# Storing one 4 MiB block in two transfers of 16 KB rows instead of one of 32 KB rows

## Chip, cores and metric

One core of one Trainium2 chip runs the program. The metric is the device time of one execution in microseconds (us). The span of a profile is about 1.3 us shorter than the time of the same execution.

## The reference

A DoRA forward pass: a 256 x 256 weight is adapted by a product of rank 16, its columns are normalised and scaled, and a large x is multiplied by it.

```python
W_adapted = W + scale * (lora_A @ lora_B)                      # 256 x 256
W_norm = np.sqrt(np.sum(W_adapted ** 2, axis=0, keepdims=True) + 1e-8)
W_final = W_adapted / W_norm * m
y = x.reshape(-1, 256) @ W_final                               # 32768 x 256, fp32 in and out
```

x and y are 33.6 MB each. They are what the time goes into.

## The kernel before

x is cut into 8 blocks of 4096 rows (32 KB a partition, 4 MiB). Five block buffers hold x on the chip. A block has 8 groups; a group g is one product of 512 rows, and its result is written by ScalarE over x in the same buffer. Loads are issued by the sync engine, stores by ScalarE. Each entry of `stores` is (first group, groups, rows of 1 KB in one transfer, product behind which it is issued).

```python
F = NBLK - XBUFS          # 3
G = F * CH                # 24: first group of block 3
stores = [(b * CH, CH, CH * J, 19 + b) for b in range(F - 1)]           # blocks 0, 1
stores += [(G - CH, 3, 3 * J, G), (G - 5, 5, 5 * J, G)]                 # block 2
FIRST = len(stores)
stores += [(G, 4, J, G + 3), (G + 4, 1, J, G + 4)]                      # block 3: rows of 4 KB
stores += [(G + 5, CH - 5, (CH - 5) * J, 44), (G + CH, CH, CH * J, 44)] # rest of 3; block 4
stores += [(b * CH, CH, CH * J, (b + 1) * CH - 1) for b in range(F + 2, NBLK - 1)]  # 5, 6
stores += [(g0, cnt, cnt * J, g0 + cnt - 1) for g0, cnt in units[-2:]]  # two halves of 7
# ... (transfer cuts an entry into pieces and issues each)
    for r in range(0, cnt * J, rows):
        here = x_bufs[b % XBUFS][:, c * J + r : c * J + r + rows, :]
        there = unit[:, (g0 - u0) * J + r : (g0 - u0) * J + r + rows, :]
        src, dst = (here, there) if store else (there, here)
        engine.dma_start(out=dst, in_=src).then_inc(sem(name), 16)
# ... (ScalarE, for each g)
    nc.scalar.copy(out=x_bufs[b % XBUFS][:, c * J : (c + 1) * J, :], in_=y_ps[g % 2][:])  # ...
    due = [n for n in range(len(stores)) if stores[n][3] == g]
    if due:
        nc.scalar.drain().then_inc(sem("done"), 1)   # ... then waits for it
        for n in due:
            store_y(n)
# ... (the end: the sync engine waits for the late stores)
for k, s in enumerate(late):
    nc.sync.wait_ge(s, pieces(stores[FIRST + k]))
```

Of the kernel before, what the change touches and what calls it, by code (L numbers as in the profile page):

```python
# [11 lines left out]
def kernel(  # L12
# [23 lines left out]
    J = 4  # L36
# [7 lines left out]
    CH = DJ // J  # L44
# [64 lines left out]
    G = F * CH  # L109
# [6 lines left out]
    stores = [(b * CH, CH, CH * J, 19 + b) for b in range(F - 1)]  # L116
    stores += [(G - CH, 3, 3 * J, G), (G - 5, 5, 5 * J, G)]
    FIRST = len(stores)
    stores += [(G, 4, J, G + 3), (G + 4, 1, J, G + 4)]
    stores += [(G + 5, CH - 5, (CH - 5) * J, 44), (G + CH, CH, CH * J, 44)]  # L120
    stores += [(b * CH, CH, CH * J, (b + 1) * CH - 1) for b in range(F + 2, NBLK - 1)]
    stores += [(g0, cnt, cnt * J, g0 + cnt - 1) for g0, cnt in units[-2:]]

# [272 lines left out]
```

## Time and profile before

| | before |
|---|---|
| time, median of 3 runs | 162.8 us (162.69 to 162.82) |
| span of the profile | 161.3 us |
| share of the DMA engines' span, loads and stores | 49.2% and 48.9% |
| last issue by ScalarE | 131.15 us |
| landing of block 4, of the last store | 132.1 us, 161.2 us |

Three things have to be known to read what follows. The DMA row of the slices gives the mean busy share of the 16 DMA engines in tenths. In a timeline the columns are the start in us, the duration in us, the engine, the source line, the operation, the operands, how many were merged, and in brackets the idle time before and what ended it. In a DMA view "us to landing" runs from an issue to the moment when all 16 engines have told that their part is written. The prediction shows the lines themselves.

### The profile page before, as it was taken

To read this page: it belongs to the slowest core of one execution; us is meant where nothing else is said; L and a number is where in the kernel's file an instruction comes from. 1 tells how busy PE (TensorE), PEld (TensorE's weight loads), DVE (VectorE), ACT (ScalarE), POOL (GpSimd) and SP (SyncE) were. 2 spreads that over 40 slices of the span, in tenths; PEclk is the share of its full clock that TensorE was granted. 3 is DMA by queue.
4 is the path that set the end of the run, shared out by engine and by line. 5 is a ranking of instruction groups with operands and counts; after the bars stand their busy time and mean duration, and the time that the engine had idled before them with its cause. 6 is when DMAs were issued, how large, how long until landed. Compare 5 with 4: busy or idle time off the path is not lost. (4 is left out here: it accounts for less than half of the span.)

```text
span 161.3 us, 2027 instructions
## 1 busy us (share of the span) xinstructions
PE 96.0 (60%) x786; PEld 84.8 (53%) x786; DVE 45.0 (28%) x44; ACT 66.0 (41%) x68; POOL 60.9 (38%) x38
## 2 busy tenths in 40 slices
PE   0795936999999720000799999989997920000000
PEld 0384925899998610000689999979977910000000
DVE  0667421435353500000214445335443300000000
ACT  3311740686777450000057676777774640000000
POOL 1045319668685000002938676755829000000000
PEclk9999996999999985555569999999999997555555
DMA  4999999999999999989999999999999999999995
GB/s 167 425 457 455 390 512 398 390 512 398 423 390 480 398 463 426 431 365 453 423 403 444 407 437 427 422 423 430 443 483 398 423 473 408 406 480 415 386 443 219
DMA packets 4645, 67.43 MB, mean 418 GB/s; under 512 B 657, under 2 KB 674, under 8 KB 1698
## 3 DMA queue, kind: packets, MB, share of 16 engines
q1 hardware_dynamic: 2304, 33.82, 49.2%
q10 hardware_dynamic: 2338, 33.59, 48.9%
q14 instruction: 3, 0.02, 0.0%
HBM read 33.85 MB, written 33.55 MB: 418 GB/s over the span
## 5 line engine op out<-in xcount | busy, mean ns | idle before, releaser
L276 ACT COPY x_sb<-y_ps 128x1024 f32<-128x1024 f32 x64 | 62.2, 1015 | 58.8 <-PE y_ps L335 57.1
L208 POOL CAST xb<-x_sb 128x2048 bf16<-128x2048 f32 x31 | 58.4, 1893 | 63.5 <-DMA x_sb<-in_x_dram 24.8
L335 PE MATMUL y_ps<-w_final,xt 128*128 128x256 bf16 x512 | 64.1, 279 | 3.9 <-PEq L311 3.8
L248 DVE COPY xt<-xt_ps 128x1024 f32<-128x1024 f32 x32 | 39.1, 1224 | 75.1 <-PE xt_ps L321 75.0
L335 PEld LDWEIGHTS y_ps<-w_final,xt 128*128 128x128 bf16 x512 | 51.0, 100 | 11.5 <-issue 4.9
L321 PE MATMUL xt_ps<-identity,xb 128*128 128x128 f32 x264 | 37.5, 290 | 24.9 <-PEq L311 24.9
L321 PEld LDWEIGHTS xt_ps<-identity,xb 128*128 128x128 f32 x264 | 32.8, 151 | 26.4 <-issue 25.9
L292 PE MATMUL y_ps<-identity,a_nat 128*16 128x128 f32 x2 | 0.6, 398 | 4.2 <-DMA a_nat<-in_lora_A_dram 4.2
L264 ACT CAST xb<-x_sb 128x2048 bf16<-128x2048 f32 x1 | 1.9, 1898 | 2.6 <-DMA x_sb<-in_x_dram 2.6
L292 PEld LDWEIGHTS y_ps<-identity,a_nat 128*16 128x16 f32 x2 | 0.1, 88 | 4.1 <-issue 4.1
L262 ACT ACT_TABLE_LOAD x1 | 1.3, 1283 | 2.4 <-issue 2.4
L238 DVE RECIPROCAL rnorm<-norm 128x256 f32<-128x256 f32 x1 | 1.8, 1752 | 1.3 <-ACT norm L268 1.3
L305 PE MATMUL y_ps<-sq,ones 128*128 128x256 f32 x4 | 2.1, 675 | 0.0
L214 POOL MEMSET xb<- 128x2048 bf16 x1 | 1.8, 1805 | 0.0
L305 PEld LDWEIGHTS y_ps<-sq,ones 128*128 128x128 f32 x4 | 1.2, 324 | 0.8 <-DVE sq L229 0.7
L301 PE MATMUL y_ps<-m_row,ones 1*128 1x256 f32 x2 | 1.2, 710 | 0.5 <-DMA m_row<-in_m_dram 0.5
L220 DVE CAST b_bf<-b_nat 16x256 bf16<-16x256 f32 x1 | 0.3, 281 | 3.3 <-DMA b_nat<-in_lora_B_dram 3.3
L301 PEld LDWEIGHTS y_ps<-m_row,ones 1*128 1x128 f32 x2 | 0.5, 305 | 1.0 <-DMA m_row<-in_m_dram 1.0
L268 ACT ACTIVATE norm<-y_ps,eps_col 128x256 f32<-128x256 f32 x1 | 0.5, 476 | 1.2 <-PE y_ps L305 1.2
L225 DVE SCALAR_TENSOR_TENSOR wa<-y_ps,w_nat 128x512 f32<-128x512 f32 x1 | 0.7, 692 | 0.8 <-PE y_ps L296 0.8
L296 PE MATMUL y_ps<-b_bf,aT 16*128 16x256 bf16 x2 | 0.6, 400 | 0.5 <-DVE aT L222 0.5
L241 DVE TENSOR_TENSOR w_final<-wam,rnorm 128x256 bf16<-128x256 f32 x2 | 0.8, 422 | 0.0
(14 smaller groups left out, 3.7 us busy)
## 6 DMA issues: line engine op xcount, KB each, us to landing
out_dram<-x_sb ACTq DMA_DIRECT2D x5, 4096.0 KB, 27.2
x_sb<-in_x_dram SPq DMA_DIRECT2D x7, 2048.0 KB, 29.6
x_sb<-in_x_dram SPq DMA_DIRECT2D x3, 4096.0 KB, 29.9
out_dram<-x_sb ACTq DMA_DIRECT2D x2, 2048.0 KB, 30.3
x_sb<-in_x_dram SPq DMA_DIRECT2D x1, 3072.0 KB, 46.1
out_dram<-x_sb ACTq DMA_DIRECT2D x2, 1536.0 KB, 19.3
out_dram<-x_sb ACTq DMA_DIRECT2D x1, 2560.0 KB, 30.7
out_dram<-x_sb ACTq DMA_DIRECT2D x5, 512.0 KB, 38.1
```

What stands on the lines that cost most here:

```text
L208: nc.gpsimd.tensor_copy(out=xb_bufs[p % NXB][:], in_=x_bufs[b % XBUFS][:, 2 * c * J : 2 * (c + 1) * J, :],).then_inc(sem("rounded"), 1)
L214: nc.gpsimd.memset(xb_bufs[NPR % NXB][:], 0.0).then_inc(sem("rounded"), 1)
L238: nc.vector.reciprocal(out=rnorm[:], in_=norm[:]).then_inc(dv, 1)
L241: i = nc.vector.tensor_mul(out=w_final[:, t], in0=wam[:, t], in1=rnorm[:])
L248: nc.vector.tensor_copy(out=xt_bufs[p % NXT][:].rearrange("p r t -> p (r t)").bitcast(FP32), in_=xt_ps[p % 2][:],).then_inc(sem("copied"), 1)
L262: nc.scalar.activation(out=warm[:], in_=eps_col[:], func=AF.Sqrt)
L264: nc.scalar.copy(out=xb_bufs[0][:], in_=x_bufs[0][:, 0 : 2 * J, :]).then_inc(sem("early"), 1)
L276: nc.scalar.copy(out=x_bufs[b % XBUFS][:, c * J : (c + 1) * J, :], in_=y_ps[g % 2][:]).then_inc(sem("room"), 1)
L301: nc.tensor.matmul(mb_ps, ones[0:1, :], m_row[:], start=True, stop=True).then_inc(pe, 1)
L305: i = nc.tensor.matmul(n2_ps, ones[:], sq[:, t, :], start=(t == 0), stop=(t == KC - 1))
L321: i = nc.tensor.transpose(xt_ps[p % 2][:, j * P : (j + 1) * P], xb_bufs[p % NXB][:, j, :].bitcast(FP32), identity[:],)
L335: i = nc.tensor.matmul(y_ps[h][:, j, :], xt_bufs[p % NXT][:, r : r + P, t], w_final[:, t, :], start=(t == 0 and (j % (J // 2)) == 0), stop ...
```

## The change

Its intent is to hand the DMA engines the store of block 4 in smaller rows, two transfers of 2 MiB instead of one of 4 MiB, so that it may interleave better with other transfers.

```diff
-    stores += [(G + 5, CH - 5, (CH - 5) * J, 44), (G + CH, CH, CH * J, 44)]
+    stores += [(G + 5, CH - 5, (CH - 5) * J, 44), (G + CH, CH, CH // 2 * J, 44)]
```

## The prediction

> **What bounds the kernel now.** I read the page from the top: busy shares, then the slices over time, then the DMA queues; after that the waits of the sync engine, and the DMA view stretch by stretch.
>
> From the page:
>
> ```profile
> span 161.3 us, 2027 instructions
> ...
> PE   0795936999999720000799999989997920000000
> ...
> ACT  3311740686777450000057676777774640000000
> ...
> DMA  4999999999999999989999999999999999999995
> ...
> DMA packets 4645, 67.43 MB, mean 418 GB/s; under 512 B 657, under 2 KB 674, under 8 KB 1698
> ...
> q1 hardware_dynamic: 2304, 33.82, 49.2%
> q10 hardware_dynamic: 2338, 33.59, 48.9%
> ```
>
> The DMA row shows 9 in every slice but the first, one 8 and the last: the 16 DMA engines have work from start to end. Loads (q1, issued by the sync engine) and stores (q10, issued by ScalarE) take 49.2% + 48.9% = 98.1% of the engines' span. PE and ACT are at 0 in the last seven slices (7 x 4.03 = 28 us): the tail is the store queue draining. The chain of waits ends at 131 us with ScalarE's last drain, so it says nothing about the last 30 us; the sync engine's waits do:
>
> ```profile
> SPq L360 <- DMA out_dram<-x_sb: 27.8, 4, 9.7
> ```
>
> This is the final wait for the late stores. So the time is bytes over DMA rate plus the start; an instruction on an engine counts only if it leaves the queue empty or changes the queue's own work.
>
> Where is block 4 in this queue? ScalarE's timeline gives the issue, the DMA view of the 0.3 us around the issue the time to landing:
>
> ```profile
> 104.49 0.86 ACTq L146 DMA_DIRECT2D out_dram<-x_sb  x2
> 105.39 1.93 ACT L276 COPY x_sb<-y_ps 128x1024 f32<-128x1024 f32 x2 [1.01 <-ACTq L282]
> ...
> 108.74 0.34 ACTq L146 DMA_DIRECT2D out_dram<-x_sb  x1
> ```
>
> ```profile
> out_dram<-x_sb ACTq DMA_DIRECT2D x1, 4096.0 KB, 27.2
> out_dram<-x_sb ACTq DMA_DIRECT2D x1, 1536.0 KB, 17.3
> ```
>
> The second of the pair of issues at 104.49 is block 4 (the first is the 12 KB rest of block 3). It is issued at about 104.86 and lands 27.2 us later, at 132.1. The rest of block 3, issued at 104.49, lands at 121.8. Packets are rows here, so block 4 moves between about 120 and 132 us. In the same way the later stores (issued 108.74, 119.27, 125.91, 131.15; 33.1, 32.2, 30.5 and 30.1 us to landing) land at 141.8, 151.5, 156.4 and 161.25: back to back, and the last one is the end of the span.
>
> **What the Trainium skill says.** Three places of the page "DMA: Bandwidth & Descriptors" bear on it.
> First, section "Queues, rings and completion order": each DMA engine goes round-robin between the queues that have work, one packet at a time. So packet size sets the share of a queue when both queues have work. The trace agrees; from 94 to 104 us, with 16 KB load rows against 4 KB store rows:
>
> ```profile
> q1 hardware_dynamic: 229, 3.49, 81.5%
> q10 hardware_dynamic: 227, 0.80, 19.6%
> ```
>
> The packets come one to one (229 to 227), the bytes four to one. This is the one mechanism by which halving a row could matter much: a 32 KB store row beside a 16 KB load row takes two thirds of an engine, a 16 KB one half.
> Second, section "Rules for kernel authors" asks for 128 partitions and at least 1 MiB a DMA for full bandwidth; both halves (2 MiB) stay above that. The trace agrees: the last two stores are 2 MiB each and run at the rate of the 4 MiB ones (below).
> Third, section "Why a DMA increments its semaphore by 16 and not by 1": every engine taking part posts one increment after its data, so a second transfer adds 16 small packets.
>
> **The change part by part.** The order of instructions differs on ScalarE only: one transfer of 128x8192 elements becomes two of 128x4096, at the same place, after the drain behind product 44. The wait at the end counts 32 instead of 16. Loads, compute and all other stores are the same.
>
> (a) Data packets. One row of 32 KB becomes two of 16 KB; each DMA engine has 128/16 = 8 rows of block 4, so 8 packets become 16. Their durations come from two stretches of the tail. From 142 to 148 us there are only 32 KB rows, and from 150.5 to 155 us only 16 KB rows, apart from completions:
>
> ```profile
> DMA packets 80, 2.62 MB, mean 437 GB/s; under 512 B 0, under 2 KB 0, under 8 KB 0
> ...
> q10 hardware_dynamic: 80, 2.62, 101.1%
> ```
>
> ```profile
> DMA packets 129, 1.88 MB, mean 419 GB/s; under 512 B 14, under 2 KB 14, under 8 KB 14
> ...
> q10 hardware_dynamic: 129, 1.88, 97.8%
> ```
>
> The first: 1.011 x 16 x 6 us / 80 = 1.213 us a row of 32 KB. The second: 0.978 x 16 x 4.5 us / (129 - 14) = 0.612 us a row of 16 KB. Splitting costs 2 x 0.612 - 1.213 = about 0.01 us a row, so 8 x 0.01 = 0.08 us on each engine. All of it lies on the path, since the store queue has no gap from there to the end.
> (b) Completion packets: one more on each engine. In the trace such a 4-byte packet takes 9 ns. Add 0.01 us.
> (c) A check against landings, which hold (a) and (b) together: the two 2 MiB stores at the end take 161.25 - 151.5 = 9.75 us for 4 MiB; the two 4 MiB stores before them take 151.5 - 132.1 = 19.4, or 9.7 each. The difference is 0.05 us, in line with 0.09.
> (d) One more issue on ScalarE. Issues in a row cost from about 0.4 us (start) to 1.25 us (59.46: three in 3.80 us). So the copy that began at 105.39 starts 0.4 to 1.25 us later. PE then waits for room in its result buffer, and the store of block 5 is issued later than 108.74, by 110 at most; the queue reaches it only at about 131 us. Twenty microseconds of slack. What is left of the delay meets GpSimd's wait for loads:
>
> ```profile
> 112.39 3.73 POOL L208 CAST xb<-x_sb 128x2048 bf16<-128x2048 f32 x2 [1.97 <-DMA x_sb<-in_x_dram]
> 119.86 3.73 POOL L208 CAST xb<-x_sb 128x2048 bf16<-128x2048 f32 x2 [3.75 <-DMA x_sb<-in_x_dram]
> ```
>
> 1.97 us and 3.75 us of idle time, ended by a load, take up 1.25 us. After 112.4 us the compute should run as before. No load is issued after 86.1 us, so none can be delayed. Cost on the path: 0.
>
> Sum: 0.05 to 0.09 us on 162.8, about 0.04%; nothing is removed. Predicted time: 162.8 + 0.07, rounded to 162.9.
>
> **The rivals.**
> First, the share of the queues. If block 4's rows moved beside loads, smaller rows would let loads arrive sooner and compute end sooner. For it: block 4 is issued at 104.9 us, when the last two loads (issued at 85.28 and 85.65; the last lands at about 119.8) are not done. Against it: stores go in order, and ahead of block 4 stand the 4 KB rows of block 3 and its 12 KB rest, which lands only at 121.8. From 118.5 to 119.5 us the view shows what is left of loads:
>
> ```profile
> q10 hardware_dynamic: 33, 0.41, 95.2%
> q1 hardware_dynamic: 12, 0.00, 0.7%
> ```
>
> q1's 12 packets are all under 512 B, so they are completions. The last load row has been moved before the first row of block 4 starts. There is nothing to share, and even if a few rows met, the total of bytes is the same and compute (done at 131) has 30 us to spare: 162.7 to 163.0.
> Second, ScalarE could block on the new issue because too many transfers are queued, and hold up the drain of the result buffers. For it: issues of 1.25 us exist. Against it: at 62 us seven stores were queued or moving and issue still took 1.25 us, at 105 us it would be five or six. Even 10 us of blocking would leave the store of block 5 issued before the queue needs it: 162.9.
> Third, a better time from a more even end. The last slice shows 5 tenths: the 16 engines don't end together. From the landings per engine, the middle ones finish the last store at 159.8 and the slowest at 161.2, a lag of 1.4 us that was 0.8 at 121.8. If 16 KB rows suffered less from whatever slows that engine during block 4, up to 0.6 us could come back; if they suffered more, as much could be lost. Nothing says which: 162.3 to 163.4.
> Fourth, writes with a gap between rows (16 KB pieces of a 32 KB pitch) might run slower than whole blocks. Against it: the same layout is loaded at 16 KB a row, and 12 KB and 20 KB pieces are stored, with DMA shares of 99 to 101% and 423 to 429 GB/s. If the 4 MiB slowed by 10%, it would cost 1 us: 163.8. I give this 3%.
>
> **Range and chances.** The three runs of before span 0.13 us, and my sum is below that. The range is the sum plus the scatter of runs and the third rival's half: 162.4 to 163.3. Leaving the 2% band would need 3.3 us, a third of the whole time of block 4's store, and no rival gives that. Faster 1%, within 2% 98%, slower 1%.
>
> **What would show it right or wrong.** After the change, the page should show 4 issues of 2048 KB and 4 of 4096 KB on the store side, 144 packets more on q10 (128 rows and 16 completions), the same share of DMA, and the same last load at 119.8. The two halves should land near 127 and 132, the stores behind them at the same times to 0.2 us, and ScalarE's last issue at 131 as before. A delay at 105 should be gone by GpSimd's cast at 112.4. I am wrong if a slice after 120 us falls under 9 in the DMA row before the last, if the last load moves, or if 16 KB rows of block 4 take more than 0.63 us.

## The result

| | before | after |
|---|---|---|
| median of 6 runs | 162.75 us (162.69 to 162.82) | 162.88 us (162.54 to 163.19) |
| ratio, 95% interval | | 1.0008 (0.9993 to 1.0023) |

The ratio is the mean time of one kernel's runs over that of the other's in the same rounds, so it isn't quite the ratio of the medians. Executions over 1.5% slower than the fastest of the same kernel are left out of the means. The two kernels are the same within what runs can tell: by the interval the change costs between -0.1 and +0.4 us.

The page of the kernel after, the lines that answer to those of before:

```profile
span 161.5 us, 2028 instructions
...
DMA  4999999999999999989999999999999999999995
...
DMA packets 4789, 67.43 MB, mean 417 GB/s; under 512 B 673, under 2 KB 690, under 8 KB 1714
...
q1 hardware_dynamic: 2304, 33.82, 49.2%
q10 hardware_dynamic: 2482, 33.59, 49.0%
```

The DMA row is the same in each slice. The store queue has 2482 - 2338 = 144 packets more, 128 of data and 16 completions of 4 bytes (673 - 657), and its share rose by 0.1 of a point.

ScalarE around block 4, timeline of the kernel after:

```profile
103.95 1.31 ACTq L146 DMA_DIRECT2D out_dram<-x_sb  x3
105.30 1.93 ACT L276 COPY x_sb<-y_ps 128x1024 f32<-128x1024 f32 x2 [1.47 <-issue]
```

Three issues take 1.31 us where two took 0.86: the added issue cost 0.45 us, and the copy behind it waited 1.47 us instead of 1.01. The DMA view gives 23.0 us to landing for the first half, issued at 104.31, so 127.3; in the trace the second half lands at 132.2.

Did that delay reach GpSimd, which feeds the products? Its timeline after:

```profile
112.85 3.73 POOL L208 CAST xb<-x_sb 128x2048 bf16<-128x2048 f32 x2 [2.38 <-DMA x_sb<-in_x_dram]
120.66 3.73 POOL L208 CAST xb<-x_sb 128x2048 bf16<-128x2048 f32 x2 [4.08 <-DMA x_sb<-in_x_dram]
```

No. Both casts still wait for a load, with more idle time than before (1.97 and 3.75 us).

One thing did move: ScalarE's last issue comes at 133.62 us instead of 131.15. The last load explains 0.80 us of these 2.47: it lands at 120.61 instead of 119.81 (the end of GpSimd's second wait above). The table of stretches shows the rest; the columns are the stretch, its length, then busy time and count of PE, PEld, DVE, ACT and POOL, then the granted clock of PE, the DMA share and GB/s. Before:

```profile
120.00:131.00 11.00, 8.74 (x79) 7.64 (x76) 2.65 (x3) 7.51 (x8) 5.34 (x3) 1.00 1.04 447
```

After:

```profile
120.00:131.00 11.00, 8.89 (x67) 7.58 (x65) 2.56 (x3) 5.63 (x6) 5.48 (x3) 0.84 1.05 449
```

PE was granted 0.84 of its clock in this stretch of the second trace and did 67 matmuls in 8.89 us instead of 79 in 8.74. The DMA share is the same. I don't put either part down to the change. In `after_again`, a second trace of the same kernel, and in `tail16`, which has two splits more, the clock in this stretch is 1.00, and ScalarE's last issue (132.82 and 131.71) comes 11.34 us behind the landing of the last load (121.48 and 120.37), just as in the kernel before; in the first trace of the kernel after it comes 13.01 behind. And the last load lands at 119.6 to 120.0 in the three stall runs below, which have the split too. The store queue never notices either.

**Landings in the trace.** Runs of one kernel spread over 0.1 to 1.3 us, and over more than 2 in `tail16` and `tail4`, which is more than the effect in question. The 16 engines' landings in one trace are finer. They are read from the packed trace itself, since the views give only the last of the 16. Of each store they give the middle engine (the ninth of the 16 landings; of the last store of `even4`, which lands in 39 parts, the eighth from the end) and the slowest. Times in us; "rest of 3" is the 12 KB store that stands just ahead of block 4:

```
run           block 4 stored as      rest of 3   block 4   block 6   last store      last store, slowest
                                     middle      middle    middle    middle          (behind the middle)
before        1 x 32 KB rows         121.02      130.69    150.16    159.83          161.22  (1.39)
after         2 x 16 KB rows         121.27      130.99    150.38    160.07          161.50  (1.43)
after_again   2 x 16 KB rows         121.08      130.79    150.21    159.90          162.11  (2.22)
tail16        2 x 16 KB, also 5, 6   121.22      130.92    150.51    160.24          161.57  (1.33)
rows4         2 x 4 KB, also 5, 6    121.36      131.39    151.41    161.13          162.22  (1.09)
tail4         8 x 4 KB, also 5, 6    121.51      131.52    153.71    168.54          169.25  (0.71)
even4         1 x 32 KB rows         121.56      131.27    150.65    160.59          161.87  (1.28)
```

The kernel after is 0.25 us late at 121 us already, and 0.24 us late at the end. The first row of block 4 starts at 120.71 us instead of 120.49, and the middle engine lands its loads 0.3 us later from 87 us on (87.65 against 87.37), long before block 4 is issued, so the change did not make it late. What lies between is the part that the change can touch: 159.83 - 121.02 = 38.81 us before, 160.07 - 121.27 = 38.80 after, 38.82 in the second trace of the kernel after. From the rest of block 3 to block 4 it is 9.67 us before and 9.71 in the same layout of the run `even4`; 9.72, 9.71 and 9.70 where block 4 is split into 16 KB rows (9.70 to 9.72 in the three stall runs). So the split costs at most about 0.05 us. In these two traces the rows of block 4 don't meet loads: the last load row ends at 118.96 us before and 119.79 after, ahead of block 4's first row.

### The profile page after: what moved, and what is told of

Its sections match the earlier page's. It is cut to its first block, busy times and chain, and to the rows that moved or that the text cites. A ratio compares the mean times of both kernels' runs of the same rounds, so it can differ in the third digit from the quotient of the medians.

```text
span 161.5 us, 2028 instructions
## 1 busy us (share of the span) xinstructions
PE 98.5 (61%) x786; PEld 86.4 (53%) x786; DVE 44.9 (28%) x44; ACT 66.1 (41%) x68; POOL 60.7 (38%) x38
## 3 DMA queue, kind: packets, MB, share of 16 engines
q10 hardware_dynamic: 2482, 33.59, 49.0%
## 5 line engine op out<-in xcount | busy, mean ns | idle before, releaser
L335 PE MATMUL y_ps<-w_final,xt 128*128 128x256 bf16 x512 | 65.8, 284 | 4.6 <-PEq L311 4.6
L335 PEld LDWEIGHTS y_ps<-w_final,xt 128*128 128x128 bf16 x512 | 52.1, 102 | 13.1 <-issue 5.7
L321 PE MATMUL xt_ps<-identity,xb 128*128 128x128 f32 x264 | 38.2, 294 | 24.0 <-PEq L311 24.0
L321 PEld LDWEIGHTS xt_ps<-identity,xb 128*128 128x128 f32 x264 | 33.3, 153 | 25.4 <-issue 24.9
## 6 DMA issues: line engine op xcount, KB each, us to landing
x_sb<-in_x_dram SPq DMA_DIRECT2D x7, 2048.0 KB, 29.8
```

The source lines that it names most:

```text
L321: i = nc.tensor.transpose(xt_ps[p % 2][:, j * P : (j + 1) * P], xb_bufs[p % NXB][:, j, :].bitcast(FP32), identity[:],)
L335: i = nc.tensor.matmul(y_ps[h][:, j, :], xt_bufs[p % NXT][:, r : r + P, t], w_final[:, t, :], start=(t == 0 and (j % (J // 2)) == 0), stop ...
```

## The experiments

Eleven runs were made, all with correct results, on two chips, each beside runs of the kernel before on the same chip; "before" below is those. The theory is that of the prediction: the queue is never empty, a split costs packet time only, ScalarE has some 20 us of slack. The rivals: the share of the queues, ScalarE's issue time, the slowest engine.

### after_again: the kernel after, once more

No edit. The first six runs spread over 0.65 us, those of before over 0.13.

> The changed kernel itself once more. Theory (a split costs only packet time, about 0.09 us an engine): 0.0 to 0.2 us over the kernel before, ratio 1.000 to 1.001. Rival (the split made the end unsteady: the first six runs spread over 0.65 us, those of before over 0.13): the spread is again over 0.4 us and the ratio may lie outside of this. If the spread is that of chance, it comes back near 0.2 to 0.3 us.

Measured: 162.91 us (162.3 to 163.46) against 162.92 for before (162.55 to 163.34, 11 runs), ratio 0.9992 (0.9968 to 1.0016). The spread is 1.16 us, over the 0.4 that the rival named and far from the 0.2 to 0.3 of chance. But the kernel before spreads over 0.79 us here, so a wide spread doesn't single out the split; its narrow 0.13 in the first six runs was the exception. Both intervals, this and the first, hold a ratio of 1.

### tail16: three blocks split

```diff
-    ..., (G + CH, CH, CH * J, 44)]
-    stores += [(b * CH, CH, CH * J, (b + 1) * CH - 1) for b in range(F + 2, NBLK - 1)]
+    ..., (G + CH, CH, CH // 2 * J, 44)]
+    stores += [(b * CH, CH, CH // 2 * J, (b + 1) * CH - 1) for b in range(F + 2, NBLK - 1)]
```

> The split in three blocks instead of one: blocks 4, 5 and 6 all stored in 16 KB rows, none of which meets a load. Theory of packet time: 3 x (8 x 0.01 + 0.01) = 0.27 us over the kernel before, so 163.0; 432 packets more on the store queue. Rival (a gap between transfers, or slower writes where rows leave gaps of 16 KB): more than 1 us over, growing with the number of split blocks. Rival (smaller rows even out the end): under 162.6.

Measured: 163.18 us (162.71 to 165.03), ratio 1.0033 (0.9991 to 1.0075). One run of 165.03 widens the interval, which holds both 1 and the expected 1.0017. The trace says more: from the rest of block 3 to the end, middle engine, 160.24 - 121.22 = 39.02 us against 38.81, so 0.21 us for three blocks, near the 0.27 expected. No gap of a microsecond, no gain.

### tail4 and rows4: a large dose, and what it was made of

tail4 cuts blocks 4, 5 and 6 into 8 transfers of 4 KB rows each.

```diff
-    ..., (G + CH, CH, CH * J, 44)]
-    stores += [(b * CH, CH, CH * J, (b + 1) * CH - 1) for b in range(F + 2, NBLK - 1)]
+    ..., (G + CH, CH, J, 44)]
+    stores += [(b * CH, CH, J, (b + 1) * CH - 1) for b in range(F + 2, NBLK - 1)]
```

> A larger dose of packets: blocks 4, 5 and 6 stored in 4 KB rows, 8 transfers each. A 4 KB packet took 0.159 us and a 32 KB one 1.213 in the trace before, so 8 x 0.159 - 1.213 = 0.059 us a row, 8 rows an engine and block, and 7 more completions of 0.009: 0.53 us a block, 1.6 us in all, so 164.3 (ratio 1.010). ScalarE issues 21 transfers more; at up to 1.25 us each it falls behind by up to 26 us less what waits take up, and its last issue comes at 140 to 150 us instead of 131, still before the queue is empty. Rival (ScalarE's issue time counts): over 168. Rival (row size does not count at all): 162.6 to 163.0.

Measured: 169.33 us (167.68 to 170.63); the four fast runs, 167.68 to 169.93, give a ratio of 1.0351 (1.0307 to 1.0396), so 5.7 us more. This is 4 us more than packet time allows, and what the rival of ScalarE (over 168) said. The profile fell in a slow run (170.63), so I take the mechanism from it and not the size. ScalarE's timeline:

```profile
103.77 13.73 ACTq L146 DMA_DIRECT2D out_dram<-x_sb  x9
117.54 1.93 ACT L276 COPY x_sb<-y_ps 128x1024 f32<-128x1024 f32 x2 [13.88 <-issue]
...
121.71 8.21 ACTq L146 DMA_DIRECT2D out_dram<-x_sb  x8
...
142.05 7.90 ACTq L146 DMA_DIRECT2D out_dram<-x_sb  x8
...
155.87 0.34 ACTq L146 DMA_DIRECT2D out_dram<-x_sb  x1
```

ScalarE spends 13.73 + 8.21 + 7.90 = 29.8 us in issues. Inside the first group the trace has six issues of 0.45 to 0.47 us in a row, then one of 3.24 and one of 7.17: with many stores queued an issue waits. Block 6 lands at 153.8 and the next store is issued at 155.87 only, so the queue is empty between; the last one is issued at 162.29. This is the second rival of the prediction come true, with seven added issues a block instead of one.

rows4 takes the packets and leaves the issues: the same 4 KB rows, but in two transfers a block (even and odd pieces).

```diff
+            if store and cnt == CH and b > F:       # on top of tail16
+                here, there = (
+                    t.rearrange("p (a h c) k -> p a h (c k)", h=2, c=J)[:, :, r // rows, :]
+                    for t in (x_bufs[b % XBUFS], unit)
+                )
```

> Blocks 4, 5 and 6 in 4 KB rows, as in the run that came out 6.5 us longer, but in two transfers each (the even and the odd 4 KB pieces), so ScalarE issues three transfers more instead of 21. If the 6.5 us were packets: again 168 or more. If they were ScalarE's issue (its issue times of 3.2 and 7.2 us when many transfers were queued): only the packets are left, 0.3 us a block by the landings of that run, 0.5 by the packets' own durations: 0.9 to 1.6 us in all, ratio 1.005 to 1.010. In the trace ScalarE has no issue above 1.5 us near 105 us, unless the queue's limit counts rows: then it has.

Measured: 163.46 us (163.18 to 163.86), ratio 1.0041 (1.0019 to 1.0063), so 0.3 to 1.0 us longer by the interval, and clear of no change. The trace: 161.13 - 121.36 = 39.77 us, 0.96 more than before, or 0.32 a block. So packet time is a real cost and it grows with the number of rows, and the packets account for about 1 of the 5.7 us of tail4. The rest was ScalarE. Yet ScalarE blocked here as well:

```profile
108.44 15.10 ACTq L151 DMA_DIRECT2D out_dram<-x_sb  x2
123.58 1.93 ACT L281 COPY x_sb<-y_ps 128x1024 f32<-128x1024 f32 x2 [15.26 <-issue]
...
146.54 0.34 ACTq L151 DMA_DIRECT2D out_dram<-x_sb  x1
```

Two issues took 15.1 us, with only five older stores queued, but of many rows. So what fills up isn't a count of transfers alone. Three of the four long issues of the two runs ended 0.1 to 0.9 us after an older store had landed (110.31 after 110.17 and 117.50 after 116.59 in tail4, 123.54 after 122.66 here), which looks like a wait for room, but doesn't show what is counted. ScalarE's last issue came 15 us later than in the kernel before, at 146.54, and it cost nothing: the store ahead of it landed only at 157.4. One block of 15 us lies inside the slack; three in a row, 30 us in all, did not.

### stall15, stall30, stall98: how much slack ScalarE has

The kernel after, with n spare copies on ScalarE just behind the issue of block 4 (n = 32, 63, 98). They write scratch that nothing reads any more.

```diff
+        if g == 44:
+            spare = [wa[:, 0], wa[:, 1], wam[:, 0], wam[:, 1], m_all[:], rnorm[:], norm[:]]
+            for k in range(n):
+                if k >= 7:
+                    nc.scalar.wait_ge(sem("stall"), k - 6)
+                nc.scalar.copy(out=spare[k % 7], in_=sq[:, 0]).then_inc(sem("stall"), 1)
```

> The changed kernel with ScalarE held for about 15 us (32 spare copies of 128x256) just behind its issue of block 4. Theory (the store queue holds 22 us of work there that ScalarE's issue has to keep ahead of): ratio to the kernel before 0.998 to 1.003, although the last issue comes about 10 to 15 us later than 131. Rival (ScalarE's time counts): 5 to 15 us longer.

> The same with about 30 us (63 spare copies). Now ScalarE issues block 5 at about 139 us, 7 to 9 us after the queue ran empty at about 131. Theory: a hole of that size in the DMA row near 132 us, and the end 7 to 11 us later, 170 to 174. If the queue has no such limit: 163. If all of ScalarE's time counts: 30 us more than the kernel before, and 15 us more than the run with 15.

I had mis-sized the copies: in a row they came every 0.306 us, so the two runs held ScalarE for about 10 and 19 us, not 15 and 30. stall15: 163.51 us against 162.81, ratio 1.0031 (1.0004 to 1.0058), at the edge of what was expected; block 5 was issued 11 us later, at 119.68. In its trace the stretch from the rest of block 3 to the end takes 38.86 us, 0.05 over the kernel before, so what the runs add isn't in the queue's work; the slowest engine was 2.07 us behind the middle one in that trace. stall30: 163.54 us, ratio 1.0051 (1.0012 to 1.0090). Its timeline:

```profile
128.61 0.34 ACTq L146 DMA_DIRECT2D out_dram<-x_sb  x1
...
140.26 0.34 ACTq L146 DMA_DIRECT2D out_dram<-x_sb  x1
```

Block 5 is issued at 128.61, in time (the middle engine finishes block 4 at 130.77). Block 6 is issued at 140.26, when the middle engine finishes block 5 at 140.45. Block 6 then takes 10.89 us to land behind it instead of 9.7: 1.2 us of hole. With 19 us the slack is just used up.

> The changed kernel with ScalarE held behind its issue of block 4 for about 30 us (98 spare copies, which came every 0.306 us in the earlier run, so that 63 of them held it only 19.3 us). ScalarE is free again at about 135 us and issues block 5 at about 139.3; the queue is empty from about 130.8, and the earlier run had 1.2 us from an issue to its first packet. Theory (22 us of queued work, and what exceeds them is paid): 10 us of hole before block 5, 2 more before block 6, so the end about 12 us later: 174 to 176, ratio 1.06 to 1.08. Rival (the slack is not the queue's, and the late compute is absorbed elsewhere): under 168. Rival (all of it counts): 30 us more.

Measured: 174.91 us, ratio 1.0729 (1.0698 to 1.0759), inside the expected 174 to 176. The page of this run:

```profile
DMA  5999989899999999899999999999990059589996
```

and its timeline:

```profile
140.16 0.34 ACTq L146 DMA_DIRECT2D out_dram<-x_sb  x1
...
151.80 0.34 ACTq L146 DMA_DIRECT2D out_dram<-x_sb  x1
```

A slice is 4.34 us here. The two slices of 0, from 130 to 139 us, and a part of the 5 behind them are the hole before block 5; the one before block 6 is in the second 5 and the 8 behind it. By the landings of the middle engine block 5 takes 19.9 us and block 6 11.7 instead of 9.7 each, so the holes are 10.2 and 2.0 us. Of 30 us that ScalarE was held, 12 reached the end. So the slack behind block 4's issue is 18 to 20 us. An added issue of 0.45 us is nowhere near it. One number of the expectation was misread: from an issue to its first packet it is 0.84 us here and in stall30, and the 1.2 us were the hole there.

### meet32 and meet16: the change where it does meet loads

Block 4 is issued behind product 40 instead of 44, ahead of the rest of block 3, so that its rows are moved while the last load is. meet32 keeps 32 KB rows, meet16 has 16 KB rows.

```diff
-    ..., (G + CH, CH, CH * J, 44)]
+    ..., (G + CH, CH, CH * J, 40)]            # meet32
+    ..., (G + CH, CH, CH // 2 * J, 40)]       # meet16
```

> The kernel before, but block 4 (still one transfer of 32 KB rows) is issued behind product 40 instead of 44, so that it stands ahead of the rest of block 3 and its rows meet the last load, from about 114.5 us. Theory (packets one to one, bytes conserved): 16 KB of load for 32 KB of store, so the last load lands at about 124 to 127 instead of 119.8 and ScalarE's last issue comes at about 135 to 138 instead of 131; the end stays within 0.3 us of the kernel before. Rival (the share of the loads decides the end): 3 us or more longer.

> The same with block 4 in two transfers of 16 KB rows, which is the change made at a place where it does meet loads. Theory: 16 KB of load for 16 KB of store, so the last load lands at about 121 to 123, 3 to 5 us sooner than with 32 KB rows at the same place, and ScalarE's last issue is that much sooner; the end is within 0.3 us of the kernel before. Rival (share decides the end): 3 us or so faster than its twin with 32 KB rows.

Measured: meet32 163.14 us, ratio 1.0018 (0.9995 to 1.0042); meet16 162.81 us, ratio 1.0005 (0.9981 to 1.0029); before 162.81. GpSimd's wait for the last load, timeline of meet32:

```profile
124.46 3.73 POOL L208 CAST xb<-x_sb 128x2048 bf16<-128x2048 f32 x2 [6.61 <-DMA x_sb<-in_x_dram]
```

and of meet16:

```profile
120.16 3.73 POOL L208 CAST xb<-x_sb 128x2048 bf16<-128x2048 f32 x2 [4.12 <-DMA x_sb<-in_x_dram]
```

With the rows halved the last load lands 2.2 us sooner on the middle engine (119.7 instead of 121.9). On the slowest, for which GpSimd waits, it is 4.3 us (120.1 instead of 124.4), but not all of that is the row size: in the trace of meet32 the slowest engine was 2.2 us behind the middle one in the load before already (114.07 and 111.85), in that of meet16 0.5. ScalarE's last issue comes at 133.11 instead of 137.95. The load of meet16 came sooner than I expected (121 to 123), and that of meet32 is inside 124 to 127 only by its slow engine; that part of the load was already done on many engines would explain it, but isn't shown. So the row size does set the share between queues, where they meet. It still doesn't set the end: in this pair the compute is done 4.8 us sooner and the queue has no use for that.

### b3rows16: larger rows where they meet loads

The first half of block 3 in one transfer of 16 KB rows instead of four of 4 KB.

```diff
-    stores += [(G, 4, J, G + 3), (G + 4, 1, J, G + 4)]
+    stores += [(G, 4, 4 * J, G + 3), (G + 4, 1, J, G + 4)]
```

> The other direction: the first half of block 3, which is stored beside loads, in one transfer of 16 KB rows instead of four of 4 KB; the rest as before. Theory of packet time: 8 rows an engine, each 4 x 0.159 - 0.611 = 0.025 us less, and 3 completions fewer: 0.2 us less, so 162.5 to 162.6. In the trace the loads lose share (one 16 KB load row for one 16 KB store row instead of for one 4 KB row): the load that landed at 88.1 lands later, this store lands near 95 instead of 110, and the last load is hardly moved, since the bytes are the same. Rival (the share decides the end): the compute starts later and the end moves by over 1 us.

Measured: 162.77 us, ratio 0.9999 (0.9972 to 1.0025). In the trace this store lands at 95.3 instead of 110.0, the load of 88.1 at 89.8, and the last load at 126.8 instead of 119.8, against my "hardly moved": block 4's 32 KB rows and block 3's rest now meet it. ScalarE's last issue comes at 139.6. All of it is inside the slack. The expected gain of 0.2 us is too small for these runs to show.

### even4: less work for the slowest engine

One engine ends 1 to 2 us behind the middle one and sets the end. I tried to relieve it, on a guess which one it is.

```diff
+        if n == len(stores) - 1:      # the kernel before, last store in three transfers
+            for p, r in ((slice(0, P), slice(0, 3 * J)), (slice(0, 120), slice(3 * J, 4 * J)),
+                         (slice(120, P), slice(3 * J, 4 * J))):
+                nc.scalar.dma_start(out=unit[p, r, :], in_=data[p, r, :]).then_inc(sem(f"store{n}"), 16)
```

> The kernel before with the last store (four products, 16 KB rows) in three transfers: 12 KB rows of all 128 partitions, then the last 4 KB of partitions 0 to 119, and of partitions 120 to 127. If the engine that ended 1.0 to 2.2 us behind the middle one in every profile so far is the one that gets no row of a transfer of 120 partitions[...], it has eight 4 KB packets less, 1.3 us, and the end is set by the second slowest, 0.5 to 1.3 us behind the middle: 0.3 to 0.9 us faster than before, ratio 0.994 to 0.998. If it is another one: the same or 0.1 to 0.3 us slower, and one engine lands its share 1.3 us earlier than the middle ones do.

Measured: 162.79 us, ratio 1.0003 (0.9981 to 1.0025). The trace has 39 landings of data for these three transfers, 16 + 15 + 8, so the transfers did use 16, 15 and 8 engines, but the last landing is at 161.87, as late as in other traces. It gave no gain; the slowest engine is probably not the one left out. Which it is, and why it is slow, stays open: the trace doesn't name the engine of a packet. In the traces it lags by 0.7 to 2.2 us whatever the row size, so it isn't a matter of the change. No version beat both kernels.

## Why the prediction was right

It said 162.9 us within 162.4 to 163.3 and 98% for the same within 2%; 162.88 was measured. That the two agree to 0.02 us is luck: the six runs spread over 0.65 us, and their interval holds no change at all. What the runs do bear out is that nothing large happens, and the reasons given for it. By its own steps:

- **The bound.** Shown. The queue is never empty in the kernel after, and its stretch from the rest of block 3 to the end grew by more than packet time only where ScalarE came too late and left it empty (stall98, tail4, and by 1.2 us stall30).
- **(a) to (c), packet time, 0.05 to 0.09 us.** The order of size is shown, the number for one block is at the edge of what a trace resolves: at most about 0.05 us, then 0.21 for three in one trace, 0.96 for three in 4 KB rows. The sum of packet durations over-estimates: it gave about 0.5 us a block for 4 KB rows, the landings 0.32. Packets of that size overlap a little: their share in rows4 from 132 to 150 us is 102.5%. The check by landings in (c), 0.05, was the better one.
- **(d), the added issue.** It took 0.45 us, the lower end of 0.4 to 1.25, and GpSimd's wait took it up, as said. The slack of 20 us is measured at 18 to 20.
- **First rival, the share.** Right to rule out, for the reason given: the rows don't meet. Where they were made to meet, the load moved by 2.2 us on the middle engine and the end did not.
- **Second rival, ScalarE blocked by a full queue.** Ruled out rightly for this change, on a weak argument. I took it that seven stores, "queued or moving" at 62 us with issues of 1.25 us, show room enough; tail4 has an issue of 3.2 us behind nine stores, and rows4 one of 10 us behind five, two of them of many rows. The part of the argument that held was the other one: that even 10 us of blocking would be free. rows4 shows 15 us free.
- **Third rival, the uneven end.** No effect of the split: the slowest engine is 1.43 us behind the middle one after (2.22 in the second trace), 1.39 before (1.28 in even4).
- **Fourth, rows with gaps between them.** Shown wrong: tail16 and rows4 cost no more than packet time.
- **What the profile was to show.** 144 packets more, four stores of 2 MiB and four of 4, halves near 127 and 132, no slice under 9, 16 KB rows of 0.611 us: as said. "ScalarE's last issue at 131 as before" failed (133.6), for the two reasons above. The stores behind block 4 land 0.3 us later and not within 0.2, as late as its loads are from 87 us on. The cast at 112.4 came at 112.85, and the last load at 120.6 instead of 119.8, which the prediction had named as a sign that it is wrong. It was a poor sign: 0.3 us of it is the lateness from 87 us on (middle engine 119.4 after, 119.1 before), the rest is the slowest engine, and in the stall runs, with the same split, the last load lands at 119.6 to 120.0.

## What to carry to other kernels

Before splitting a transfer, look at when its rows are moved, not when it is issued: if the other queue is done by then, row size has nothing to share out and only packet time is left. Where the queue sets the end, count how far the issuing engine runs ahead of it, for that is what added issues may use up; many rows queued can make one issue last 10 us. For effects of a tenth of a microsecond, take the interval between two landings of the middle engine in one trace; it repeats to a few hundredths where whole runs scatter by half a microsecond.

## What the Trainium skill lacked or had wrong

- "DMA: Bandwidth & Descriptors", section "Queues, rings and completion order", has nothing on the issue of a transfer waiting when much is queued. "Perfetto Trace Analysis", section "DMA Instruction — HWDGE (DVE, Sync)", names a descriptor buffer that can fill, but gives no size of it and no time that an issue waits. Here an issue on ScalarE took 0.34 to 0.5 us near 105 us, but 3.2 and 7.2 us as the seventh and eighth of 4 KB rows behind three older stores, and 10.0 us behind two transfers of 4 KB rows (32 rows an engine each) and three older ones, then 5.1 for the next. What exactly fills up stays open. The first of these sections also gives a packet only in descriptors, some 9 to 17, which a trace doesn't show; here the turn was one row: from 94 to 104 us 213 load rows of 16 KB and 195 store rows of 4 KB alternated (229 packets to 227 with the 48 completions).
- "DMA: Bandwidth & Descriptors", section "Measured", has times of whole loads only. Store rows here took 0.159 us for 4 KB, 0.611 for 16 KB and 1.213 for 32 KB; 4 MiB landed in 9.66 to 9.75 us in 32 KB rows (before, after, after_again and even4), in 9.67 to 9.73 in 16 KB rows but for one block of 9.87 in tail16, and in 9.94 to 10.08 in 4 KB rows (rows4).
- The same page, section "Latency and other measured facts", speaks of two engines usually slower than the others and puts it down, as a guess, to the software path. Here all data moved on the hardware path, and one engine still ended 0.7 to 2.2 us behind the middle one. No run here shows which one.
